# Neighbourhood attention in column order of the grid, inside a one-core backbone kernel

## The chip, the cores and the metric

The kernel runs on one core of a Trainium2 chip, as one program with one launch. The metric is device time in microseconds. Its profile comes from one more execution, recorded by the hardware's profiler.

The core's engines run side by side and meet at semaphores: TensorE (PE, with its weight loads listed as PEld), VectorE (DVE), ScalarE (ACT), GpSimd (POOL) and SyncE (SP), which issues most DMAs. A DMA can also be issued from ACT's queue. Each engine takes its instructions in the order in which they were written. TensorE writes its results to eight banks, each of 128 partitions by 512 fp32 values; the other engines read them from there.

## The reference, cut to what matters

A backbone of two layers works on 256 latent tokens (a grid of 4 rows by 64 columns), 256 context tokens and a width of 2048. Layer 0 has 16 attention heads of 128 and 32 state-space (SSD) heads side by side, then one output projection; layer 1 is a gated short convolution. The change is in the attention of layer 0. With 4 rows the row window of 8 holds all rows, so a query sees 16 of 64 columns, in each of the 4 rows, and all of the context:

```python
def neighbourhood_attention(q, k, v, k_ctx, v_ctx, rpb):
    ...
    kh = min(NA_KH, rows)
    col_start = jnp.clip(col - NA_KW // 2, 0, GRID_W - NA_KW)
    in_win = (col[None, :] >= col_start[:, None]) & (col[None, :] < col_start[:, None] + NA_KW)
    ...
    def row_block(r):
        ...
        s_lat = jnp.einsum('bqhd,bkhd->bhqk', qr, kb).astype(jnp.float32) * scale + bias.astype(jnp.float32)
        s_lat = jnp.where(mask, s_lat, -jnp.inf)
        s_ctx = jnp.einsum('bqhd,bkhd->bhqk', qr, k_ctx).astype(jnp.float32) * scale
        pr = jax.nn.softmax(jnp.concatenate([s_lat, s_ctx], axis=-1), axis=-1).astype(v.dtype)
        return (jnp.einsum('bhqk,bkhd->bqhd', pr[..., :kh * GRID_W], vb)
                + jnp.einsum('bhqk,bkhd->bqhd', pr[..., kh * GRID_W:], v_ctx))
```

The bias comes from a table `rpb` by row and column distance. Queries and keys are normalised per head first; the output is multiplied by a SiLU gate.

## The kernel before, in words

All products are made of three matmuls: each fp32 operand is split into a high part in the rounded format fp32r and a low part (the remainder), and high x high, high x low and low x high are added in a bank. Weights stream from memory through five buffers `raw` of 512 KB. ScalarE casts the high half (L420), VectorE subtracts the low half (L427), into one of three places `w`; later in the kernel further buffers serve as places too. A load is issued on SP (L381, L383) when a `raw` buffer comes free, in the order of the list of loads; between them go the loads of `adaT`, rows of the modulation matrix that VectorE multiplies (L823).

The order of the work is made by a planner in the kernel. The projections are written out as a fixed sequence of matmuls. Everything else is a generator that yields, before each step, the engine and the tiles that it needs; after each small group of matmuls `pump()` emits those steps whose inputs and engine are ready by the planner's own estimates. There are three queues: `urgent` (turning, gates, SSD inputs), `side` (heads and SSD groups, in the order in which they were put there) and `back` (the modulation). So a step that is moved shifts others.

Attention runs in four blocks of four heads (a = 0 to 3). `do_qk` projects queries (256 latent tokens, two tiles of 128) and keys (512 tokens: four tiles, two latent and two context). `kq_gen` normalises them and turns them with TensorE, tile by tile, four heads to a bank (L199); ScalarE copies the high part out of the bank (L994, L998), VectorE makes the low part (L996, L1000). Tokens keep their order, row by row. `v_gen` copies the projected values, tile by tile, to `Vt` (L1012).

`head_gen` is one head. It loads the bias from a table `rpbs` that was spread out in DRAM at the start, with four small DMAs (L1039), and adds the column mask (L1044). For each of two query tiles, `score` makes three matmuls of 512 columns (all 256 latent and 256 context keys; L195 is the line of every matmul). `top` adds bias and finds the maximum (L1057), ScalarE takes the exponential (L1062), `scale_` divides (L1067). TensorE turns the probabilities; their high and low parts go to `PH` and `PL` (L1099, L1101). The head's values are split into `VH` and `VL` (L1110, L1112), and twelve matmuls of 256 columns (four key tiles by three) give the output, which is multiplied by the gate (L1122). `put_mix` sends it to DRAM, or directly to the high and low buffers `mix` of the output projection (L944, L946) when that is near. `mix_gen` fetches those that went to DRAM back (L1561, L1562).

After block a come the SSD projections of two groups, `do_ssd(a)`; its group steps are `group_gen`. Block 3 differs: its gates and values are projected after `do_ssd(3)`, directly ahead of the output projection, whose first use of the last four heads' outputs (mix 12 to 15) is at the end of its first pass.

Of the kernel before, what the change touches and what calls it, by code (L numbers as in the profile page):

```python
# [31 lines left out]
for _name, _w in (("ident", 128), ("sel", 2), ("mhalf", 32), ("strip", 384), ("mask", 64)):  # L32
    _coff[_name] = (_n, _n + _w)
    _n += _w
# [107 lines left out]
def kernel(ctx: ExitStack, tc, x, cx, ada0, w0, adaT, w_in, w_out, sc_in, sc_out, rpb, small, const,  # L142
# [209 lines left out]
    ident, strip, mask, mhalf = C_("ident"), C_("strip"), C_("mask"), C_("mhalf")  # L352
# [200 lines left out]
    for a in range(1, 4):  # L553
        qk = [(w_in, CQ(a), 512), (w_in, CK(a), 512)]
        gv = [(w_in, CG(a), 512), (w_in, CV(a), 512)]
        for j_ in qk + gv + ssd_cols(a) if a < 3 else qk + ssd_cols(a) + gv:
            q_proj(*j_)
# [356 lines left out]
    got.add(("V", 0))  # L914
# [13 lines left out]
    rpbs = drt([16, 64, 320], "rpbs")  # L928
    E(DMA.dma_start(rpbs, bass.AP(tensor=rpb.tensor, offset=76, ap=[[465, 16], [0, 64], [1, 320]])))
    dcol = P_("dcol")  # L930
    for b_ in bias:
        E(G.memset(b_[:, 2, :], 0.0))
# [26 lines left out]

    def kq_gen(key, a, ps, nt, stat, dst, low, banked):  # L960
# [23 lines left out]
        for t in range(nt):  # L984
            yield W_("PE", kns[t], nb=1)
            pt = bank()
            for h in range(4):
                turn(pt[:, h * 128:(h + 1) * 128], kns[t][:, h * 128:(h + 1) * 128])

            o = slice(t * 128, (t + 1) * 128)  # L990
            yield W_("ACT", pt)
            if key == "K":
                give(free_t, kns[t])
                E(S.copy(dst[:, :, o], four(pt)))  # L994
                yield W_("DVE", dst[:, :, o])
                E(V.tensor_tensor(out=low[:, :, o], in0=four(pt), in1=dst[:, :, o].bitcast(F32), op=ALU.subtract))  # L996
            else:
                E(S.mul(dst[:, :, o], four(pt), gqk))  # L998
                yield W_("DVE", dst[:, :, o])
                E(V.scalar_tensor_tensor(out=low[:, :, o], in0=four(pt), scalar=gqk, in1=dst[:, :, o].bitcast(F32),  # L1000
                                         op0=ALU.mult, op1=ALU.subtract))
                give(free_t, kns[t])
            give(free_b, pt)
        got.add((key, a))

    def v_gen(a, ps):
        yield when(lambda: not (attn[0] < 8 * a))
        for t in range(4):

            on_dve = a == 3 and t % 2  # L1010
            yield W_("DVE" if on_dve else "ACT", ps[t])
            E(V.tensor_copy(Vt[:, t, :], ps[t]) if on_dve else S.copy(Vt[:, t, :], ps[t]))  # L1012
            give(free_b, ps[t])
        got.add(("V", a))
# [14 lines left out]
    b0 = rpbs[0, :, :]  # L1029
# [3 lines left out]
    def head_gen(a, h):  # L1033
# [4 lines left out]
        for r in range(4):  # L1038
            E(DMA.dma_start(bt[64 * (r % 2):64 * (r % 2) + 64, r // 2, :].rearrange("p (a b) -> p a b", a=4),  # L1039
                            bass.AP(tensor=b0.tensor, offset=b0.offset + hd * 64 * 320 + (7 - r) * 31 - 61,  # L1040
                                    ap=[[319, 64], [31, 4], [1, 64]])))
        yield W_("DVE", bt)
        bv = bt[:, 0:2, :].rearrange("p q (r c) -> p (q r) c", c=64)
        E(V.tensor_tensor(out=bv, in0=bv, in1=mask.unsqueeze(1).to_broadcast([128, 8, 64]), op=ALU.add))  # L1044
        sps = {}

        def score(qt):
# [3 lines left out]
            mm(ps, QT[:, h, o], KL[:, h, :], False, False)  # L1051
            mm(ps, QL[:, h, o], KT[:, h, :], False, True)
            return ps

        def top(qt, ps):
            sp = sps[qt] = tmp()
            E(V.tensor_tensor_reduce(out=two(sp), in0=two(ps), in1=bt[:, 1:3, :] if qt else bt[:, 0::2, :], scale=1.0,  # L1057
# [4 lines left out]
            E(S.activation(sp, sp, AF.Exp, bias=s4[:, 2 + qt:3 + qt], scale=1.0, accum_out=s4[:, 4 + qt:5 + qt]))  # L1062

        def scale_(qt):
            sp = sps[qt]
# [49 lines left out]
        for kt in range(4):  # L1115
            mm(po[:, :256], VH[:, kt], PH[:, kt, :], kt == 0, False)
            mm(po[:, :256], VH[:, kt], PL[:, kt, :], False, False)
            mm(po[:, :256], VL[:, kt], PH[:, kt, :], False, kt == 3)
# [3 lines left out]
        E(V.tensor_tensor(out=o, in0=po[:, :256], in1=gt[:, h, :], op=ALU.mult))  # L1122
# [358 lines left out]
    Btm[0] = st([128, 2, 4, 128], "Btm", name="Btmt")  # L1481
    spawn(urgent, kq_gen("K", 0, parK, 4, statk, KT, KL, False), 4)
    spawn(urgent, kq_gen("Q", 0, psQ, 2, statq, QT, QL, True), 2)

    def do_g(a, nxt):
        psG = banks(2)
        proj(512, 256, psG, nxt)
        spawn(urgent, silu2_gen("G", a, psG, gt, lambda: attn[0] >= 8 * a and (a or ("K", 0) in got)), 1)
# [34 lines left out]
    def do_qk(a, nxt):  # L1523
# [6 lines left out]
        for h in range(4):  # L1530
            spawn(side, head_gen(a, h))

    def do_gv(a, nxt):
        do_g(a, 4)
# [9 lines left out]
    do_ssd(3, 2)  # L1544


    def mix_gen(ip):
# [11 lines left out]
        for j, i in enumerate(pair):  # L1559
            hl = st([128, 2, 256], f"hH{i}" if i < 16 else f"hL{i - 16}", F32R, name=f"mix{i}")  # L1560
            E(S.copy(hl[:, 0], m3[:, j]))  # L1561
            E(V.tensor_tensor(out=hl[:, 1], in0=m3[:, j], in1=hl[:, 0].bitcast(F32), op=ALU.subtract))  # L1562
# [490 lines left out]
```

## Time and profile before

| | |
|---|---|
| median of 3 runs | 1765.8 us (1763.58 to 1766.23) |
| the profiled execution | 1760.31 us |
| its span, first to last instruction | 1758.5 us |
| PE busy | 1736.7 us, 99% |
| DVE busy | 1223.6 us, 70% |
| ACT busy | 773.4 us, 44% |
| mean granted TensorE clock | 0.999 |
| DMA | 377.66 MB, mean 215 GB/s |

Busy time is the time in which at least one instruction of an engine runs. A matmul's row gives its own length, into which the next one already runs, so the rows' lengths add up to more than the busy time. Idle time of an engine stands with what ended it. A wait in the list of waits is that idle time, by pairs of who waited and who released. Numbers at the end of a name (bank, tmp) are left out in the profile's rows.

### The profile page before, as it was taken

What the parts mean: (1) busy time and instruction counts of PE and PEld (TensorE: products, weight loads), DVE (VectorE), ACT (ScalarE), POOL (GpSimd) and SP (SyncE); (2) the same over time, 40 slices, a digit from 0 to 9 for tenths busy, and PEclk for the clock granted to TensorE, in tenths of its full rate; (3) what the DMA queues carried; (4) which work ended last, traced back from release to release, by engine and by line L of the source; (5) the groups of instructions that cost most, each with busy time, mean ns of one, the idle gap of its engine ahead of it and who ended that gap; (6) DMA issues with size and microseconds to landing.
All of it is one profiled execution on the core that took longest, in us unless ns stands there. A gap on an engine that the chain in (4) does not pass through costs nothing.

```text
span 1758.5 us, 25025 instructions
## 1 busy us (share of the span) xinstructions
PE 1736.7 (99%) x9451; PEld 1463.1 (83%) x9451; DVE 1223.6 (70%) x1978; ACT 773.4 (44%) x1330; POOL 31.6 (2%) x28
## 2 busy tenths in 40 slices
PE   6999999999999999999999999999999999999998
PEld 4777988889888889888888898888888888888887
DVE  5666887878685878686877787787668555555554
ACT  5333544445242436343435343564446444444442
POOL 0000100001000000000000000000000000000000
PEclk9999999999999999999999999999999999999999
DMA  9987644686756767656776557768767666666563
GB/s 362 342 307 258 209 143 138 183 246 191 234 165 195 219 205 227 210 175 210 220 213 193 166 185 255 246 221 284 274 222 228 195 188 192 192 191 188 190 208 121
DMA packets 202536, 377.66 MB, mean 215 GB/s; under 512 B 32384, under 2 KB 69040, under 8 KB 202416
## 3 DMA queue, kind: packets, MB, share of 16 engines
q1 hardware_dynamic: 195152, 369.49, 65.5%
q10 hardware_dynamic: 7264, 6.58, 1.1%
q8 instruction: 74, 1.21, 0.3%
q14 instruction: 46, 0.38, 0.1%
HBM read 370.62 MB, written 6.71 MB: 215 GB/s over the span
## 4 chain that ended last, share of the span: by engine, by line
PE 94%; DMA 2%; DVE 2%; issue 1%; ACT 0%; POOL 0%; SPq 0%; ACTq 0%; DVEq 0%; POOLq 0%
PE bank L195 91%; PE bank L199 3%; DMA tmp<-dram_csr 1%; DVE w L427 1%; DMA raw<-in_ada 0%; DMA tmp<-dram_exr 0%; DMA raw<-in_adaT 0%; DVE tmp L1235 0%; ACT w L420 0%; POOL statk L572 0%; DVE mix L1562 0%; SPq L583 0%; DVE raw L823 0%; DVE tmp L603 0%; DVE Vt L1012 0%
## 5 line engine op out<-in xcount | busy, mean ns | idle before, releaser
L420 ACT CAST w<-raw 128x1024 fp32r<-128x1024 f32 x343 | 359.5, 1049 | 530.4 <-PE bank L195 447.7
L427 DVE TENSOR_TENSOR w<-raw,w 128x1024 fp32r<-128x1024 f32 x343 | 416.6, 1217 | 231.4 <-ACT w L420 230.1
L195 PE MATMUL bank<-hH,w 128*128 128x256 f32 (+1 forms) x2064 | 488.0, 324 | 1.2 <-DVE w L427 1.1
L195 PE MATMUL bank<-w,hH 128*128 128x512 f32 x1280 | 407.4, 396 | 2.7 <-ACT hH L757 2.5
L195 PEld LDWEIGHTS bank<-hH,w 128*128 128x128 f32 x2064 | 344.7, 188 | 34.2 <-DVE w L427 2.1
L195 PE MATMUL bank<-hL,w 128*128 128x256 f32 (+1 forms) x1040 | 334.3, 321 | 0.0
L195 PEld LDWEIGHTS bank<-w,hH 128*128 128x128 f32 x1280 | 237.7, 189 | 54.4 <-issue 4.0
L195 PE MATMUL bank<-w,hL 128*128 128x512 f32 x640 | 249.9, 391 | 0.1
L195 PEld LDWEIGHTS bank<-hL,w 128*128 128x128 f32 x1040 | 196.3, 189 | 14.9
L195 PE MATMUL bank<-w,h 128*128 128x512 f32 x768 | 179.7, 390 | 0.0
L823 DVE CUSTOM_DVE_ANT_0 raw<-raw,csb 128x1024 f32<-128x1024 f32 x128 | 155.4, 1219 | 26.2 <-DMA raw<-in_adaT 24.0
L195 PEld LDWEIGHTS bank<-w,h 128*128 128x128 f32 x768 | 143.6, 188 | 29.6
L195 PEld LDWEIGHTS bank<-w,hL 128*128 128x128 f32 x640 | 120.5, 188 | 25.4 <-DVE hL L763 0.6
L195 PE MATMUL bank<-w,mix 128*128 128x512 f32 x588 | 138.3, 391 | 0.9 <-DVE w L427 0.9
L195 PEld LDWEIGHTS bank<-w,mix 128*128 128x128 f32 x588 | 109.5, 188 | 24.0 <-DVE w L427 1.3
L1235 DVE SCALAR_TENSOR_TENSOR tmp<-bank,cwh,tmp 128x508 f32<-128x508 f32 (+1 forms) x96 | 71.0, 744 | 1.8
L195 PE MATMUL bank<-KL,h 128*128 128x512 f32 x264 | 63.8, 389 | 0.0
L427 DVE TENSOR_TENSOR KL<-raw,KL 128x1024 fp32r<-128x1024 f32 x32 | 39.1, 1223 | 33.1 <-ACT KL L420 33.1
L427 DVE TENSOR_TENSOR wL<-raw,wH 128x1024 fp32r<-128x1024 f32 x31 | 37.9, 1224 | 33.5 <-ACT wH L420 33.4
L427 DVE TENSOR_TENSOR QL<-raw,QT 128x1024 fp32r<-128x1024 f32 x32 | 39.2, 1224 | 29.8 <-ACT QT L420 29.8
L195 PEld LDWEIGHTS bank<-KL,h 128*128 128x128 f32 x264 | 49.5, 188 | 10.2
L195 PE MATMUL bank<-QT,h 128*128 128x512 f32 x168 | 56.2, 391 | 0.0
(291 smaller groups left out, 1984.7 us busy)
## 6 DMA issues: line engine op xcount, KB each, us to landing
raw<-in_w_in SPq DMA_DIRECT2D x196, 512.0 KB, 3.9
raw<-in_adaT SPq DMA_DIRECT2D x128, 512.0 KB, 4.8
raw<-in_sc_in SPq DMA_DIRECT2D x128, 512.0 KB, 3.8
raw<-in_w_out SPq DMA_DIRECT2D x64, 512.0 KB, 5.0
raw<-in_ada SPq DMA_DIRECT2D x34, 512.0 KB, 6.9
raw<-in_sc_out SPq DMA_DIRECT2D x32, 512.0 KB, 4.1
PT<-in_ada SPq DMA_DIRECT2D x16, 512.0 KB, 6.9
raw<-in_w SPq DMA_DIRECT2D x16, 512.0 KB, 6.1
```

The costliest lines, as they stand in the source:

```text
L195: E(T.matmul(o, l, r, start=start, stop=stop, skip_group_check=True))
L199: E(T.transpose(o, i, ident if k == 128 else ident[:k, :k]))
L420: E(S.copy(H, v))
L427: E(V.tensor_tensor(out=Lo, in0=v, in1=H.bitcast(F32), op=ALU.subtract))
L823: E(V.tensor_tensor_reduce(out=raw, in0=raw, in1=csb, scale=1.0, scalar=0.0, op0=ALU.mult, op1=ALU.add, accum_out=gp[:, h, m:m + 1]))
L1235: E(V.scalar_tensor_tensor(out=do, in0=di, scalar=cwh[:, 32 * k + ch:32 * k + ch + 1], in1=do, op0=ALU.mult, op1=ALU.add))
```

## The change

Tokens are ordered column by column of the grid inside attention (token = 4 x column + row), so that a tile of 128 queries is 32 columns by 4 rows. The keys a tile can see then lie in 40 neighbouring columns, 160 tokens, and the key order becomes: latent columns 0 to 31, context, latent columns 32 to 63. Tile 0 needs keys 0 to 415 of 512, tile 1 needs 96 to 511.

- `kq_gen` turns the two latent tiles of two heads into one bank, and writes them in the new order: two runs of 64 elements with a step of four elements. Context tiles are turned as before.
- The values' latent tiles go to DRAM in two pieces each and come back in the new order (`turn_v`, `turned_v`), on SP; for block 0 this runs right after the first projections (`first_v`).
- Scores have 416 columns. The 96 others of the probabilities are set to zero by VectorE. In the value products two of four key tiles have 160 columns.
- The bias table is laid out by the host in the final order, one load of 128x672 per head; the mask is added in three pieces.
- The heads of block 3 are put into `side` after SSD groups 6 and 7, not before them.
- In `mix_gen` the low part is a step of its own.

How that shows in the engines' order. On TensorE, where the keys of block 0 are turned while the gates are projected (`hH` times `w`; `tmp` holds normalised keys, `const` the identity), before:

```order
L195 MATMUL bank_84<-hH_994,w_97 128x256
L199 MATMUL bank_88<-const,tmp_65 128x128 x4
L195 MATMUL bank_82<-hH_994,w_97 128x256
L195 MATMUL bank_82<-hL_999,w_97 128x256
L195 MATMUL bank_82<-hH_994,w_97 128x256 x2
L195 MATMUL bank_82<-hL_999,w_97 128x256
L195 MATMUL bank_82<-hH_994,w_97 128x256
L199 MATMUL bank_85<-const,tmp_73 128x128 x4
L195 MATMUL bank_84<-hH_1096,w_95 128x256
```

And now:

```order
L195 MATMUL bank_82<-hH_994,w_97 128x256
L199 MATMUL bank_88<-const,tmp_65 128x2x64
L199 MATMUL bank_88<-const,tmp_73 128x2x64
L199 MATMUL bank_88<-const,tmp_65 128x2x64
L199 MATMUL bank_88<-const,tmp_73 128x2x64
L199 MATMUL bank_85<-const,tmp_65 128x2x64
L199 MATMUL bank_85<-const,tmp_73 128x2x64
L195 MATMUL bank_84<-hH_1096,w_95 128x256
```

The two banks are filled behind one another once both tiles are normalised, four turns in each, instead of one bank per tile.

On TensorE in the output projection's first pass, at the last heads (`mix` is the projection's left side, KT and QT are scores, PH and VH value products), before:

```order
L195 MATMUL bank_83<-KL,QT 128x512
L195 MATMUL bank_83<-KT,QL 128x512
L195 MATMUL bank_88<-w_96,mix_8971 128x512 x3
L195 MATMUL bank_86<-w_97,mix_9045 128x512 x3
L195 MATMUL bank_89<-w_97,mix_9045 128x512 x3
L195 MATMUL bank_86<-w_97,mix_9048 128x512 x3
L195 MATMUL bank_89<-w_97,mix_9048 128x512 x3
L195 MATMUL bank_84<-w_95,mix_9045 128x512 x3
L195 MATMUL bank_87<-PH,VH 128x256
```

And now:

```order
L195 MATMUL bank_82<-PH,VL 128x256
L195 MATMUL bank_82<-PH,VH 128x160
L195 MATMUL bank_82<-PL,VH 128x160
L195 MATMUL bank_82<-PH,VL 128x160
L195 MATMUL bank_83<-w_95,mix_9227 128x512 x3
L195 MATMUL bank_87<-KT,QT 128x416
L195 MATMUL bank_87<-KL,QT 128x416
L195 MATMUL bank_87<-KT,QL 128x416
```

Scores and value products are narrower, and the last head's scores come later: 66 matmuls stand between the last value product and the first use of mix 12, where 174 stood.

On SP, at the values of block 3 in the same pass (`raw` are weight loads, `csr` rows of the SSD groups), before:

```order
L383 DMA raw_91<-in_w_out 128x2x512
L383 DMA raw_94<-in_w_out 128x2x512
L1039 DMA bias_159<-dram_rpbs 64x4x64 x4
L383 DMA raw_93<-in_w_out 128x2x512
L1039 DMA bias_160<-dram_rpbs 64x4x64 x4
L1391 DMA tmp_65<-dram_csr 128x2x256
```

And now:

```order
L383 DMA raw_94<-in_w_out 128x2x512
L960 DMA dram_vd<-Vt 64x512 x4
L383 DMA raw_92<-in_w_out 128x2x512
L1432 DMA tmp_72<-dram_csr 128x2x256
L1432 DMA tmp_71<-dram_csr 128x2x256
L383 DMA raw_91<-in_w_out 128x2x512
L383 DMA raw_93<-in_w_out 128x2x512
L965 DMA Vt<-dram_vd 128x2x512
```

The values' writes and their read now stand among the weight loads, and the bias loads of block 3 (one per head) stand elsewhere.

The diff, cut to its core:

```diff
+    vd = drt([256, 512], "vd")
...
+    def turn_v(t):
+        for r in range(2):
+            yield W_("SP", Vt[:, t, :])
+            E(DMA.dma_start(vd.rearrange("(c r) n -> c r n", r=4)[:, 2 * t + r, :], Vt[64 * r:64 * r + 64, t, :]))
+    def turned_v(a):
+        yield W_("SP", vd)
+        E(DMA.dma_start(Vt[:, 0:2, :], vd.rearrange("(t p) n -> p t n", p=128)))
+        got.add(("V", a))
...
     def kq_gen(key, a, ps, nt, stat, dst, low, banked):
...
-        for t in range(nt):
+        for hp in (0, 2):
+            yield W_("PE", kns[0], kns[1], nb=1)
+            pt = bank()
+            for k in range(2):
+                o = pt[:, k * 256:k * 256 + 256].rearrange("p (c r) -> p r c", r=4)
+                for t in range(2):
+                    turn(o[:, 2 * t:2 * t + 2, :], kns[t][:, (hp + k) * 128:(hp + k + 1) * 128])
...
+        for t in range(2, nt):
             yield W_("PE", kns[t], nb=1)
...
     def v_gen(a, ps):
...
+            if t == 1:
+                for k in range(2):
+                    yield from turn_v(k)
+        yield from turned_v(a)
...
+    BLOCKS = ((1, 2, slice(0, 256)), (2, 3, slice(0, 256)), (0, 0, slice(0, 160)), (3, 1, slice(96, 256)))
...
     def head_gen(a, h):
...
-        for r in range(4):
-            E(DMA.dma_start(bt[64 * (r % 2):64 * (r % 2) + 64, r // 2, :].rearrange("p (a b) -> p a b", a=4),
...
+        bf = bt.rearrange("p a b -> p (a b)")[:, :672]
+        E(DMA.dma_start(bf, rpb[hd]))
...
-            mm(ps, QT[:, h, o], KT[:, h, :], True, False)
+            mm(ps[:, :416], QT[:, h, o], KT[:, h, k_], True, False)
...
+            E(V.memset(sp[:, 0:96] if qt else sp[:, 416:512], 0.0))
...
-        for kt in range(4):
-            mm(po[:, :256], VH[:, kt], PH[:, kt, :], kt == 0, False)
+        for i, (kt, vt, q_) in enumerate(BLOCKS):
+            mm(po[:, q_], VH[:, vt], PH[:, kt, q_], i == 0, False)
...
     def do_qk(a, nxt):
...
-        for h in range(4):
+        for h in range(4 if a < 3 else 0):
             spawn(side, head_gen(a, h))
...
     do_ssd(3, 2)
+    for h in range(4):
+        spawn(side, head_gen(3, h))
...
     def mix_gen(ip):
...
             E(S.copy(hl[:, 0], m3[:, j]))
+            yield W_("DVE", hl[:, 0])
             E(V.tensor_tensor(out=hl[:, 1], in0=m3[:, j], in1=hl[:, 0].bitcast(F32), op=ALU.subtract))
```

More of the change, by code (lines that the diff above doesn't have):

```diff
@@ L31 @@
 _n = 0
-for _name, _w in (("ident", 128), ("sel", 2), ("mhalf", 32), ("strip", 384), ("mask", 64)):
+for _name, _w in (("ident", 128), ("sel", 2), ("mhalf", 16), ("mid", 16), ("strip", 384), ("mask", 64)):
     _coff[_name] = (_n, _n + _w)
@@ L988, in kq_gen @@
                 turn(pt[:, h * 128:(h + 1) * 128], kns[t][:, h * 128:(h + 1) * 128])
-            o = slice(t * 128, (t + 1) * 128)
+            o = slice(t * 128 - 128, t * 128)
             yield W_("ACT", pt)
[L992 to L1002, printed above, removed]
+            give(free_t, kns[t])
+            E(S.copy(dst[:, :, o], four(pt)))
+            yield W_("DVE", dst[:, :, o])
+            E(V.tensor_tensor(out=low[:, :, o], in0=four(pt), in1=dst[:, :, o].bitcast(F32), op=ALU.subtract))
             give(free_b, pt)
```

91 lines of the change are left out of this document (62 added, 29 removed).

## The prediction

> **What bounds the kernel now.** I read the page first (busy shares and chain), then the list of TensorE's own waits, then groups of instructions by shape, then narrow timelines.
>
> ```profile
> span 1758.5 us, 25025 instructions
> PE 1736.7 (99%) x9451; PEld 1463.1 (83%) x9451; DVE 1223.6 (70%) x1978; ACT 773.4 (44%) x1330; POOL 31.6 (2%) x28
> PE 94%; DMA 2%; DVE 2%; issue 1%; ACT 0%; POOL 0%; SPq 0%; ACTq 0%; DVEq 0%; POOLq 0%
> ```
>
> TensorE (PE) is busy 99% of the span and is 94% of the chain that ended last. What it waits for, in total and longest:
>
> ```profile
> PE bank L195 <- DMA raw<-in_ada: 10.8, 1, 10.8
> PE bank L195 <- ACT hH L757: 2.5, 2, 1.4
> PE bank L195 <- DVE w L427: 2.0, 3, 0.9
> PE bank L199 <- ACT half L724: 1.0, 2, 0.5
> PE bank L199 <- ACT x L613: 0.3, 1, 0.3
> PE bank L199 <- POOL r L1664: 0.3, 1, 0.3
> PE bank L195 <- DVE gt L789: 0.2, 1, 0.2
> ```
>
> The first two, the fourth and the fifth rows are the opening (first load, first norm). The change starts after it, with the first turning of keys near 208 us. So behind the opening at most about 2.5 us of named waiting is left to win (2.0 + 0.3 + 0.2), and the time follows the matmuls that PE must issue. What one costs is its distance to the next, not its length in a row (matmuls overlap). One long run of 512 columns, from the chain, and one of 256, from busy time by stretches:
>
> ```profile
> 1235.80 68.75 PE bank L195 x303
> 297.91:320.03 22.12, 21.93 (x193) 1.00 0.50 149
> ```
>
> 512 columns: 68.75/303 = 0.227 us. 256 columns: 22.12/193 = 0.115 us, at a granted clock of 1.00. The difference is 0.112 us per 256 columns, 0.44 ns per column.
>
> **The change part by part.** Scores. Each of 16 heads has two query tiles of three matmuls, 96 in all, and their moving side shrinks from 512 to 416 columns.
>
> ```profile
> L195 PE MATMUL bank<-KT,QT 128*128 128x512 f32 x32 | 13.1, 408 | 0.0
> L195 PE MATMUL bank<-KT,QL 128*128 128x512 f32 x32 | 12.5, 391 | 0.0
> L195 PE MATMUL bank<-KL,QT 128*128 128x512 f32 x32 | 12.5, 391 | 0.0
> ```
>
> 96 columns x 0.44 ns = 42 ns less each, x 96 = 4.0 us. All of it is on PE's path, and 416 columns (0.185 us) stay far above the 0.115 us that shorter matmuls reach anyway.
>
> Values. Each head has 12 matmuls of 256 columns; six become 160 wide, 96 in all.
>
> ```profile
> L195 PE MATMUL bank<-PL,VH 128*128 128x256 f32 x64 | 17.9, 280 | 0.0
> 402.18 0.53 PEld L195 LDWEIGHTS bank<-const,half 128*128 128x128 f32 x4
> 402.63 0.19 PEld L195 LDWEIGHTS bank<-hH,w 128*128 128x128 f32 x1
> ```
>
> By columns alone a 160-wide one would take 0.073 us: another 42 ns x 96 = 4.0 us. But each matmul also has its own weight load. The second and third rows show four loads for matmuls of one single column: they start 402.18 to 402.63, 0.45 us for four, 0.112 us apart, although almost nothing is streamed. If PV's loads are as slow, a 160-wide matmul cannot follow sooner than 0.112 us, and the gain is 96 x 3 ns = 0.3 us. Ends: 0.3 and 4.0 us. I take 0.3, since these loads are the nearest row (the same 128x128 of 4 bytes, at the same clock).
>
> [...]
>
> Turning. Keys and queries are turned by as many 128-column instructions as before (16 for keys, 8 for queries in each of 4 blocks). But 64 of them (32 for latent keys, 32 for queries) now write two runs of 64 elements with a step of four elements in the bank. No matmul of the old trace writes with a step, so the price is unknown.
>
> ```profile
> 1235.36 0.44 PE bank L199 x4
> L199 PE MATMUL bank<-const,tmp 128*128 128x128 f32 x356 | 50.5, 272 | 0.0
> ```
>
> A packed turn takes 0.44/4 = 0.11 us. Ends: 0 (same pace; a gain has no reason, as the elements stay 128), and 64 x 0.11 = 7.0 us if each takes twice as long. I take 0: a turn delivers 128 elements in 0.11 us, 1.2 per ns, half the 2.2 per ns of the 256-column stream above, so the bank is written with room to spare.
>
> VectorE and ScalarE. The score reduction (L1057, 32 times, 0.685 us at 512 elements) loses 96 elements, the scaling (0.487 us) and the exponential as well. Against it stand 32 zero fills of 96 elements and 32 more, smaller, additions of the mask.
>
> ```profile
> L1057 DVE CUSTOM_DVE_ANT_0 tmp<-bank,bias 128x512 f32<-128x512 f32 x16 | 11.0, 686 | 2.5 <-PE bank L195 2.5
> L1067 DVE TENSOR_SCALAR tmp<-tmp,s 128x512 f32<-128x512 f32 x32 | 15.6, 487 | 1.1
> L1044 DVE TENSOR_TENSOR bias<-bias,const 128x512 f32<-128x512 f32 x16 | 11.0, 685 | 0.5 <-DMA bias<-dram_rpbs 0.5
> L1122 DVE TENSOR_TENSOR half<-bank,gt x16: 408/423/425, 270.9 to 1170.2; 128x256 f32<-128x256 f32 x16
> L1060 DVE TENSOR_SCALAR s<-s x32: 153/154/156, 253.1 to 1155.1; 128x1 f32<-128x1 f32 x32
> ```
>
> From 0.685 at 512 and 0.423 at 256 an element costs 1.02 ns with a fixed 0.16. Reductions: 32 x 0.098 = -3.1 us. Scaling: (0.487-0.154)/511 x 96 x 32 = -2.0. Mask: per head 0.29+0.23+0.29 instead of 0.685, +2.0 in all. Fills: between 0.154 and 0.26 us each, +4.9 to +8.3. Net +2 to +5 us on an engine that is idle 535 us. I cost it at nothing: what hides it is the ready weights, below. The split of copy and subtraction in the mixing step (L1561, L1562) lets VectorE do other work where it waited for ScalarE:
>
> ```profile
> 1118.16 0.76 DVE L1562 TENSOR_TENSOR mix<-tmp,mix 128x256 fp32r<-128x256 f32 x2 [0.88 <-ACT mix L1561]
> 1122.46 1.89 PE L195 MATMUL bank<-w,mix 128*128 128x512 f32 x7 [0.91 <-DVE w L427]
> ```
>
> The second row is one of the three waits of PE for VectorE, just behind such a stall. It may vanish or move: 0 to -0.9 us, and I take 0, because the new order packs the same work (value copies, mixing, group 3's scores) into the same stretch.
>
> Queues. SyncE (SP) issues the weights in order. It loses 64 bias loads and one table copy, and gains 16 bias loads (336 KB each), 16 writes (128 KB) and 4 reads (512 KB) of the turned values: 29 fewer.
>
> ```profile
> L1039 SPq DMA_DIRECT2D bias<-dram_rpbs x64: 573/614/2243, 223.6 to 1139.2; - x64
> dram_mixd<-half ACTq DMA_DIRECT2D x24, 128.0 KB, 3.1
> raw<-in_w_in SPq DMA_DIRECT2D x196, 512.0 KB, 3.9
> L1012 ACT COPY Vt<-bank x10: 573/590/608, 477.9 to 1120.8; 128x512 f32<-128x512 f32 x10
> ACT w L420 <- PE bank L195: 458.1, 223, 5.8
> SPq L383 <- DVE w L427: 601.5, 237, 7.0
> ```
>
> At 0.614 us an issue that frees about 18 us of SP, which no one waits for. The new risk is a wait in that queue: the writes wait for the value copies, the read waits for the writes (3.1 us by the nearest row, the same 128 KB), and all weight loads stand behind. In the order of group 3, three weight loads stand between writes and read, each for 12 matmuls of 0.227 = 2.7 us of PE work, so the writes have landed by then. And PE is covered: ScalarE waited 458 us for PE to hand back places, so split weights lie ready, and SP waited 601 us for free buffers, so loads run ahead. Cost 0; if the cover is gone, the 3.1 us of a landing come out as a wait of PE for a weight's low half (L427 of before).
>
> Last heads. Their scores now come behind the SSD groups, and group 3's values are late by the round trip (3.1 + 3.9 us, the row of a load of the same 512 KB, and queueing). In the order, 66 matmuls stand between the last value product and the first use of head 12's output, where there were 174: 66 x 0.227 = 15.0 us against a tail (product with the gate 0.42, copy, subtraction) of about 2 us. Cost 0; SSD outputs, which are used before them, gain the room.
>
> **The sum.** -4.0 - 0.3 = -4.3 us of PE. The profiled execution took 1760.3 us (1758.5 plus 1.8 around it) and would take 1756.0. It lies 5.5 us under the median of the runs, 1765.8, and by that median the forecast is 1761.5.
>
> **The rivals.**
> (a) Narrow value products do gain by columns: -8.0, 1757.8. Against it speaks the 0.112 us between loads; for it, that these loads feed another number format.
> (b) Writing with a step slows the 64 turns. Twice as long: +7.0 - 4.3 = +2.7, 1768.5. This is the one that can end slower: it decides from 7.8/7.0, an extra 1.1 times a turn's 0.11 us; three times as long gives +9.7, 1775.5. No row speaks for it; the pace of a turn, half the stream's, speaks against. [...]
> (c) The round trip or the late heads open waits of PE. It costs nothing until the values of group 3 are 13 us later than the order has them (15.0 - 2). From there each us late is a us of wait: 4.3 us eat the gain (1765.8), past 7.8 us it is slower, and if each of the four groups made PE wait out the 3.1 us of a landing, 12.4 us, it would be 1773.9. For it: a slack of 15 us where there was 39. Against: the 29 fewer issues and the ready weights.
> (d) The change saves nothing because other work fills the freed slots: 1765.8. Against it: PE is the chain, and the removed columns are its own.
>
> **How the numbers follow.** A change under 0.2% (3.5 us) can hardly be told from none here; the three runs shown span 2.7 us. Chances: the sum as it stands 0.48 (0.40 of it past 3.5 us, 0.08 short of it), (a) in part or full 0.15, (b) about twice 0.10, (b) beyond that 0.07, (c) small 0.06, (c) large 0.11, (d) 0.03. Faster 0.55, same 0.27, slower 0.18. The range reaches from 1756.5 ((a), with the one wait of 0.9 gone) to 1768.5 ((b) at twice).
>
> **What would show it.** In the profile after: score matmuls 128x416, with lengths about 42 ns under 391 (that is 349); value products of 160 columns that start about 0.112 us apart (a if near 0.073); groups of four stepped turns at 0.44 us (b if 0.9); TensorE's waits behind the opening still near 2.5 us, none naming the values or a weight load late behind L965 (c otherwise). The forecast is wrong if PE's busy time falls by 4 us and the span doesn't, or if the busy time itself doesn't fall.

## The result, and the profile after

The changed kernel takes 1759.7 us (median of 22 runs, 1756.5 to 1764.5), the kernel before on the same chip 1763.2 us (22 runs, 1760.1 to 1768.6). The ratio is 0.9976, 95% interval 0.9968 to 0.9984: 4.2 us less, a gain of 0.24% (by the interval 2.8 to 5.6 us; the two medians alone lie 3.5 us apart). The sum of the forecast was -4.3 us.

The profiled execution of the changed kernel says something else at first sight. Its page, with the span, the busy shares and the chain that ended last:

```profile
span 1759.6 us, 25036 instructions
PE 1733.2 (99%) x9451; PEld 1462.6 (83%) x9451; DVE 1218.6 (69%) x2042; ACT 768.1 (44%) x1330; POOL 31.4 (2%) x26
PE 94%; DMA 2%; DVE 2%; ACT 1%; issue 0%; SPq 0%; POOL 0%; DVEq 0%; ACTq 0%
```

The span is 1.1 us longer than that of the profile before (1758.5), while TensorE's busy time fell by 3.5 us (1736.7 to 1733.2). So in this pair of executions TensorE worked less and waited more. Its waits in the trace after (total us, times, longest us):

```profile
PE bank L195 <- DVE ssq L603: 10.8, 1, 10.8
PE bank L195 <- DVE w L427: 6.2, 5, 3.0
PE bank L195 <- ACT hH L757: 2.5, 2, 1.4
...
```

Row by row, with those left out (1.0 us and less), this is the list of before (the 10.8 us of the first load stand under another releaser), but for one: the waits for VectorE's low half of the weights (L427) went from 2.0 to 6.2 us. The longest, 3.0 us, lies at 679 us. The chain of work there (start, length, what):

```profile
672.92 6.64 DMA raw<-in_adaT
...
680.91 1.14 DVE w L427
...
682.09 3.03 PE bank L195 x18
```

and VectorE's step on the adaT tile, with its own idle time in brackets:

```profile
679.59 1.23 DVE L823 CUSTOM_DVE_ANT_0 raw<-raw,csb 128x1024 f32<-128x1024 f32 x1 [2.09 <-DMA raw<-in_adaT]
```

VectorE had reached the next step of the matrix-vector product (L823), whose adaT tile was 6.6 us in transfer, and stood there for 2.1 us; the weight half that TensorE needed (L427) is the next long step in its order. And the wait costs more than its 3.0 us. Busy time by stretches of the same trace (stretch, its length, busy us of TensorE with the number of matmuls, weight loads, VectorE, ScalarE, GpSimd, then the granted clock):

```profile
678.00:682.00 4.00, 1.14 (x10) 0.93 (x8) 2.41 (x5) 2.25 (x5) 1.01 (x1) 1.00 0.33 120
682.00:683.30 1.30, 1.21 (x10) 1.21 (x11) 1.30 (x3) 0.00 (x0) 1.30 (x1) 1.00 0.86 244
683.30:686.70 3.40, 3.40 (x19) 3.40 (x19) 2.90 (x5) 0.90 (x1) 1.49 (x1) 0.53 0.94 316
686.70:690.00 3.30, 3.30 (x30) 3.30 (x30) 2.78 (x5) 1.71 (x4) 0.00 (x0) 0.97 0.74 235
```

About 1.3 us after TensorE resumed, its clock was granted at 0.53 for 3.4 us: 19 matmuls where the next 3.3 us hold 30. That is another 1.3 us or so (3.40 - 19/30 x 3.30).

The steps of the forecast, in the same trace, by shape and by start:

```profile
L195 PE MATMUL bank<-KT,QT 128*128 128x416 f32 x32 | 11.8, 370 | 0.0
L195 PE MATMUL bank<-KL,QT 128*128 128x416 f32 x32 | 11.3, 352 | 0.0
L195 PE MATMUL bank<-KT,QL 128*128 128x416 f32 x32 | 11.2, 349 | 0.0
...
271.03 0.24 PE L195 MATMUL bank<-PH,VH 128*128 128x160 f32 x1
271.10 0.28 PE L195 MATMUL bank<-PL,VH 128*128 128x160 f32 x1
271.22 0.27 PE L195 MATMUL bank<-PH,VL 128*128 128x160 f32 x1
271.33 0.28 PE L195 MATMUL bank<-PH,VH 128*128 128x160 f32 x1
...
271.66 0.61 PE L199 MATMUL bank<-const,tmp 128*128 128x128 f32 x4
...
207.97 1.04 PE L199 MATMUL bank<-const,tmp 128*128 128x128 f32 x8
```

The score matmuls are 38 to 42 ns shorter than before. The second of the six narrow value products of a head starts 0.07 us after the first, the others 0.11 us apart; all six take 271.66 - 271.03 = 0.63 us. The eight turns that write with a step (the last row) take 1.04 us as a group, of which the last takes 0.27 by its own length, so they start 0.11 us apart, like packed ones.

So two questions went to the chip: whether the 4.2 us are the columns of the scores, and whose the waits are.

### The profile page after: what moved, and what is told of

Its sections match the earlier page's. It is cut to its first block, busy times and chain, and to the rows that moved or that the text cites. A ratio compares the mean times of both kernels' runs of the same rounds, so it can differ in the third digit from the quotient of the medians.

```text
span 1759.6 us, 25036 instructions
## 1 busy us (share of the span) xinstructions
PE 1733.2 (99%) x9451; PEld 1462.6 (83%) x9451; DVE 1218.6 (69%) x2042; ACT 768.1 (44%) x1330; POOL 31.4 (2%) x26
## 4 chain that ended last, share of the span: by engine, by line
PE 94%; DMA 2%; DVE 2%; ACT 1%; issue 0%; SPq 0%; POOL 0%; DVEq 0%; ACTq 0%
PE bank L195 90%; PE bank L199 3%; DMA tmp<-dram_csr 1%; DVE w L427 1%; DMA raw<-in_adaT 1%; DMA raw<-in_ada 0%; DVE raw L823 0%; DMA bias<-in_rpb 0%; ACT w L420 0%; DVE tmp L1456 0%; ACT tmp L1441 0%; DVE tmp L1445 0%; SPq L583 0%; ACT tmp L1451 0%; DVE tmp L759 0%
## 5 line engine op out<-in xcount | busy, mean ns | idle before, releaser
L420 ACT CAST w<-raw 128x1024 fp32r<-128x1024 f32 x343 | 359.1, 1049 | 519.9 <-PE bank L195 443.6
L427 DVE TENSOR_TENSOR w<-raw,w 128x1024 fp32r<-128x1024 f32 x343 | 416.5, 1218 | 232.9 <-ACT w L420 223.6
L195 PE MATMUL bank<-w,hH 128*128 128x512 f32 x1280 | 406.3, 395 | 2.7 <-ACT hH L757 2.5
L823 DVE CUSTOM_DVE_ANT_0 raw<-raw,csb 128x1024 f32<-128x1024 f32 x128 | 155.6, 1220 | 28.7 <-DMA raw<-in_adaT 23.0
L427 DVE TENSOR_TENSOR KL<-raw,KL 128x1024 fp32r<-128x1024 f32 x32 | 39.2, 1224 | 32.4 <-ACT KL L420 32.4
L427 DVE TENSOR_TENSOR QL<-raw,QT 128x1024 fp32r<-128x1024 f32 x32 | 39.2, 1224 | 29.4 <-ACT QT L420 29.3
L427 DVE TENSOR_TENSOR wL<-raw,wH 128x1024 fp32r<-128x1024 f32 x31 | 37.9, 1224 | 30.4 <-ACT wH L420 30.4
```

The lines of the kernel that those rows point to most:

```text
L195: E(T.matmul(o, l, r, start=start, stop=stop, skip_group_check=True))
L420: E(S.copy(H, v))
L427: E(V.tensor_tensor(out=Lo, in0=v, in1=H.bitcast(F32), op=ALU.subtract))
L823: E(V.tensor_tensor_reduce(out=raw, in0=raw, in1=csb, scale=1.0, scalar=0.0, op0=ALU.mult, op1=ALU.add, accum_out=gp[:, h, m:m + 1]))
```

## The experiments: what the parts are worth

All ratios are to the kernel before, on the same chip. In pv256, s512, pv32 and no_rt the planner was shown the operands and transfers of the changed kernel, so that every engine's remaining instructions stand in exactly its order; in packed they do so anyway, and before_s416 stands in the order of the kernel before. The argument by which a matmul shows the planner the old operands is left out of the diffs.

**s512: the scores wide again.**

```diff
-            mm(ps[:, :416], QT[:, h, o], KT[:, h, k_], True, False)
-            mm(ps[:, :416], QT[:, h, o], KL[:, h, k_], False, False)
-            mm(ps[:, :416], QL[:, h, o], KT[:, h, k_], False, True)
+            mm(ps, QT[:, h, o], KT[:, h, :], True, False)
+            mm(ps, QT[:, h, o], KL[:, h, :], False, False)
+            mm(ps, QL[:, h, o], KT[:, h, :], False, True)
...
-            E(V.tensor_tensor_reduce(out=two(sc), in0=two(ps[:, :416]), in1=b_, scale=1.0,
+            E(V.tensor_tensor_reduce(out=two(sc), in0=two(ps[:, span(qt)]), in1=b_, scale=1.0,
```

> The changed kernel with all 96 score products 512 columns wide again, of which the same 416 are read; every engine's instructions in the same order. If the gain is the 96 columns that each score product lost (96 x 96 x 0.44 ns), it is gone: +4.0 us, 1.000 of the kernel before (0.9990 to 1.0008). If the gain came from elsewhere (fewer waits, less VectorE work, less traffic), the time stays at 0.9976.

Measured: 0.9995 (0.9984 to 1.0005), 1762.5 us. The gain is gone. Its trace has the old lengths again (the line is one further down):

```profile
L196 PE MATMUL bank<-KT,QT 128*128 128x512 f32 x32 | 13.1, 411 | 0.0
L196 PE MATMUL bank<-KT,QL 128*128 128x512 f32 x32 | 12.5, 390 | 0.0
L196 PE MATMUL bank<-KL,QT 128*128 128x512 f32 x32 | 12.5, 390 | 0.0
```

Between 0.9976 and this lie 0.0019, 3.4 us; the forecast's 4.0 us would make 0.9999, inside the interval. The starts of matmuls say the same without the noise of whole runs: from the first score product of a query tile to the matmul behind the third, the 32 tiles take 22.5 us in the trace of before, 18.8 in that of the changed kernel and 22.5 in this one.

**before_s416: the scores narrow, alone.**

```diff
-            mm(ps, QT[:, h, o], KT[:, h, :], True, False)
-            mm(ps, QT[:, h, o], KL[:, h, :], False, False)
-            mm(ps, QL[:, h, o], KT[:, h, :], False, True)
+            mm(ps[:, :416], QT[:, h, o], KT[:, h, :416], True, False)
+            mm(ps[:, :416], QT[:, h, o], KL[:, h, :416], False, False)
+            mm(ps[:, :416], QL[:, h, o], KT[:, h, :416], False, True)
```

> The kernel before, with its 96 score products cut from 512 to 416 columns and nothing else (the last 96 keys are left out of the products; the softmax reads what stood in the bank); every engine's instructions stand in the order of the kernel before. If the columns are the gain, this alone gives it: 96 x 96 x 0.44 ns = 4.0 us, 0.9977 of the kernel before (0.9969 to 0.9986). If the gain needs the rest of the change, 1.000.

Measured: 0.9974 (0.9959 to 0.9989), 1758.4 us. The narrow scores alone, without turning, round trip, new biases or moved heads, give as much as the whole change. Taken back from the changed kernel they take the gain with them; given to the kernel before they bring it (18.5 us from start to start in its trace). That settles where the gain is, within the 2 to 3 us of each interval.

**pv256: the value products wide again.**

```diff
-            mm(po[:, q_], VH[:, vt], PH[:, kt, q_], i == 0, False)
-            mm(po[:, q_], VH[:, vt], PL[:, kt, q_], False, False)
-            mm(po[:, q_], VL[:, vt], PH[:, kt, q_], False, i == 3)
+            mm(po[:, :256], VH[:, vt], PH[:, kt, :], i == 0, False)
+            mm(po[:, :256], VH[:, vt], PL[:, kt, :], False, False)
+            mm(po[:, :256], VL[:, vt], PH[:, kt, :], False, i == 3)
```

> The changed kernel, with all twelve value products of a head 256 columns wide again (the weights are zero in the columns added, so nothing else changes); every engine's instructions stand in the same order as in the changed kernel. If a narrow value product is held up by its weight load (the forecast's term of -0.3 us; the changed kernel's trace, where the 96 products of 160 columns start 0.09 to 0.11 us apart, says up to -1.0), this gives back 0.3 to 1.0 us: 0.9978 to 0.9982 of the kernel before. If it is paid by columns (96 x 96 columns x 0.44 ns), it gives back 4.0 us: 0.9999.

Measured: 0.9977 (0.9966 to 0.9988), 1760.3 us. By the middles of the two ratios the narrow value products are worth 0.2 us, nothing that can be told from none; the 4.0 us of rival (a), which would make 0.9999, lie outside. The starts are finer: the six products of a head that are wide again take 0.69 to 0.72 us in this trace, where the narrow ones take 0.63 to 0.64, in all 16 heads. That is 0.065 us x 16, about 1.0 us.

**pv32: the narrow value products narrower still.**

```diff
+            a_ = slice(q_.start, q_.start + (256 if i < 2 else 32))
-            mm(po[:, q_], VH[:, vt], PH[:, kt, q_], i == 0, False)
+            mm(po[:, a_], VH[:, vt], PH[:, kt, a_], i == 0, False)
...
```

> The changed kernel with its 96 value products of 160 columns cut to 32 columns (this leaves out most of those products); every engine's instructions stand in the same order. If a narrow product takes as long as its weight load (0.11 us, whatever its width), the time stays within 1 us: 0.9970 to 0.9982 of the kernel before. If it is paid by columns (96 x 128 x 0.44 ns), 5.4 us go: 0.9945.

Measured: 0.9973 (0.9957 to 0.9988), 1758.6 us; 0.9945 is outside. The reason can be read in its trace, in the starts of the products of 32 columns:

```profile
271.92 0.18 PE L196 MATMUL bank<-PH,VH 128*128 128x32 f32 x1
271.94 0.26 PE L196 MATMUL bank<-PL,VH 128*128 128x32 f32 x1
272.06 0.26 PE L196 MATMUL bank<-PH,VL 128*128 128x32 f32 x1
272.17 0.26 PE L196 MATMUL bank<-PH,VH 128*128 128x32 f32 x1
...
272.50 0.65 PE L200 MATMUL bank<-const,tmp 128*128 128x128 f32 x4
```

The second comes 0.02 us after the first (0.07 at 160 columns). From there on they start 0.11 us apart, as the 160-wide ones do: each has its own weight load, and behind the second none follows sooner than 0.11 us, at 32 columns as at 160. A head's six take 0.58 us here, 0.05 less than at 160 columns, or 0.8 us in all.

**packed: the latent turns without the step.**

```diff
-                o = pt[:, k * 256:k * 256 + 256].rearrange("p (c r) -> p r c", r=4)
+                o = pt[:, k * 256:k * 256 + 256].rearrange("p (r c) -> p r c", r=4)
```

> The changed kernel with the 64 turns of the latent keys and queries written to 128 words in a row instead of to every fourth word (this leaves out their reordering into grid order; the work is otherwise the same, in the same order on every engine). If the step costs nothing, the time stays at 0.9976 of the kernel before (within 0.0008). If a stepped write makes a turn twice as long (64 x 0.109 us), this kernel is 7.0 us faster than the changed one: 0.9936; a cost of half that shows as 0.9956.

Measured: 0.9973 (0.9961 to 0.9985), 1758.9 us. The step costs nothing that can be told from none; a doubled turn (0.9936) is outside. Its first group of turns is as long as the stepped one shown above:

```profile
208.50 1.04 PE L199 MATMUL bank<-const,tmp 128*128 128x128 f32 x8
```

**no_rt: no round trip of the values.**

```diff
-            E(DMA.dma_start(vd.rearrange("(c r) n -> c r n", r=4)[:, 2 * t + r, :], Vt[64 * r:64 * r + 64, t, :]))
...
-        E(DMA.dma_start(Vt[:, 0:2, :], vd.rearrange("(t p) n -> p t n", p=128)))
```

> The changed kernel without the round trip of the latent values through DRAM (it leaves out their reordering: 16 stores and 4 loads on SP's queue); the order of all other instructions is that of the changed kernel. If the round trip is hidden, the time stays at 0.9976 of the kernel before, within 0.0008. If its stores and loads hold up the weight streams or the value products, and so feed the waits of PE behind VectorE that the changed kernel's trace shows (4.2 us more than before the change), this kernel is 2 to 4 us faster: 0.9953 to 0.9965.

Measured: 0.9987 (0.9975 to 1.0000), 1761.0 us. Nothing is gained without the 20 transfers; the middle is even above that of the changed kernel, with intervals that overlap. Its trace has 5.4 us of waits for VectorE's weight halves, so those waits are not the round trip's.

**heads_before: the last heads where they were.**

```diff
-        for h in range(4 if a < 3 else 0):
+        for h in range(4):
             spawn(side, head_gen(a, h))
...
-    for h in range(4):
-        spawn(side, head_gen(3, h))
```

> The changed kernel with the heads of the last block started ahead of the SSD groups, where the kernel before starts them. The forecast costed their move at nothing: 0.9976 of the kernel before, within 0.0008, up to the waits that a new order shifts (the changed kernel's trace has 9 us of short PE waits on VectorE behind late transfers, which may come or go with any new order: 2 us either way). If late heads cost by waits at the end, this is 2 us or more faster: below 0.9965. If their move is where the gain came from, it is slower: 0.9990 or more.

Measured: 0.9980 (0.9968 to 0.9992), 1759.8 us: no difference from the changed kernel. (The 9 us of the expectation are not in the list of waits of the changed kernel's trace: that has 6.2 for L427, this run's has 5.2.)

## The experiments: whose the waits are

**after_again and before_again: both kernels a second time, unedited, for a second trace of each.**

> The changed kernel itself, beside the two variants of this set, and to see how far its waits differ between two executions of one program. Every theory: 0.9976 of the kernel before, within 0.0010. If the 3.1 us wait at 679 us belongs to one execution (the variants with the same order showed 0.9 to 2.5 us there), this profile shows another length there; if it belongs to the order, 3 us again.

> The kernel before itself, for a second trace of it. Its first profiled execution (1760.3 us) lay 3 us under its median and showed 2.0 us of PE waits behind VectorE's weight splits, where eight executions of the changed order showed 2.0 to 6.2. If those waits are a cost of the changed order, this execution shows about 2 us again, whatever its time. If they vary from one execution to the next in the kernel before as well, this one, nearer the median, shows 4 us or more. Against itself: 1.000, within 0.001.

Measured: 0.9979 (0.9970 to 0.9988) for the changed kernel; 0.9998 (0.9987 to 1.0008) for the kernel before against itself. The waits for L427, first in the second trace of the changed kernel, with the same two steps near 679 us:

```profile
PE bank L195 <- DVE w L427: 4.0, 4, 1.7
...
678.66 1.23 DVE L823 CUSTOM_DVE_ANT_0 raw<-raw,csb 128x1024 f32<-128x1024 f32 x1 [2.00 <-DMA raw<-in_adaT]
...
681.16 0.50 PE L195 MATMUL bank<-hH,w 128*128 128x256 f32 x2 [1.00 <-DVE w L427]
```

then in the second trace of the kernel before (span 1767.6 us), with two stretches around its longest waits by busy time and clock (columns as above):

```profile
PE bank L195 <- DVE w L427: 4.0, 4, 1.5
PE bank L195 <- ACT w L420: 2.5, 2, 1.8
...
670.00:674.00 4.00, 1.86 (x13) 1.45 (x12) 3.76 (x8) 4.00 (x10) 0.00 (x0) 0.98 0.55 174
674.00:677.00 3.00, 3.00 (x22) 2.44 (x21) 2.97 (x6) 3.00 (x19) 0.00 (x0) 0.50 0.84 276
...
1126.00:1129.00 3.00, 0.57 (x2) 0.26 (x2) 3.00 (x6) 3.00 (x6) 0.00 (x0) 0.81 0.42 130
1129.00:1132.00 3.00, 3.00 (x7) 2.41 (x8) 3.00 (x7) 2.41 (x7) 0.00 (x0) 0.50 0.90 312
```

One program, two executions: the 3.0 us wait is one of 1.0 us the second time, and the clock stays at 1.00 (680 to 690 us). VectorE stood for the adaT tile both times, 2.1 and 2.0 us; but the second time it started on the tile 0.9 us earlier (678.66 against 679.59), and TensorE ran out of weights 1.0 us later (681.16 - 1.00 against 682.09 - 2.96). The kernel before, which showed 2.0 us of waits for weights in its first trace, shows 6.5 in its second, and twice a stretch at half clock (0.50) with them. So how long such a wait is belongs to the execution, and one pair of traces can't be read for it.

The place of a wait belongs to the order. The eight traces in the changed kernel's order up to there (after, after_again, no_rt, heads_before, packed, pv256, pv32, s512) all have VectorE standing 1.9 to 2.3 us for an adaT tile near 679 us (packed at 675) and TensorE waiting behind it, 0.7 to 3.0 us; all have VectorE waiting 0.8 to 1.8 us for a bias table near 408 us, with 0.5 to 2.3 us of TensorE waits behind it; and all have a TensorE wait of 0.7 to 0.8 us near 1150 us. The three traces in the order of before have one of 0.9 near 412 us, and others at places of their own: 0.9 us near 1122 in the first, 2.1 near 672 and 3.3 near 1127 in the second, none in before_s416. All waits for weights together come to 2.0 to 6.2 us in the eight, 4.5 in the mean, and to 2.0, 6.5 and 0.9 in the three, 3.1 in the mean. So the new order may cost a microsecond or so of waits; three traces don't show it, and the medians don't resolve it.

**late3, late_mix, late_all: VectorE's steps behind transfers emitted later.** If the waits come from VectorE standing behind late transfers, they must go when the planner, which writes every engine's order, expects those transfers later. (A variant with such a rule has another order on every engine, so it is no test of one wait alone.) late3 does so for the adaT tiles and the bias tables:

```diff
-            rdy += 4000 if eng == "PE" else 0
+            rdy += 4000 if eng == "PE" else 3000 if eng == "DVE" else 0
...
         E(DMA.dma_start(bf, rpb[hd]))
+        for k_ in plan.keys(bf):
+            plan.w[k_] += 3000.0
```

late_mix has this too and also

```diff
         E(DMA2.dma_start(m3[:, :n], mixd[i0:i0 + n].rearrange("b p c -> p b c")))
+        for k_ in plan.keys(m3[:, :n]):
+            plan.w[k_] += 4000.0
```

and late_all changes instead the planner's model of every transfer:

```diff
-                done = free = self.dma + 1000
+                done = free = self.dma + 3000
...
-                done = free = max(self.dma, s + 1000) + n / self.RATE + 2500
+                done = free = max(self.dma, s + 1000) + n / self.RATE + 5000
```

> The changed kernel with one more rule in the planner: VectorE's steps on the adaT tiles and on the bias tables are emitted only where the planner holds the transfer for 3 us longer done than it does now. Nothing else is edited, but every engine's order shifts with it. If the waits of PE behind VectorE (6.2 us in the changed kernel's trace, 2.0 to 5.2 us in those of its variants) come from VectorE standing in order behind late transfers, most of them go: 2 to 4 us less than the changed kernel, 0.9953 to 0.9965 of the kernel before. If they come from VectorE's load as such, the time stays at 0.9976 or rises.

> The variant late3 with the planner also holding the loads of the finished heads from DRAM on ScalarE's queue for 4 us longer. In late3's trace the waits near 410 and 679 us had shrunk to 0.7 us, but one of 2.4 us had come at 1113 us, behind an 8.6 us load of that kind. If each wait can be removed at its place, this one is 2 us less than late3: 0.996. If a shifted order brings another wait as often as it removes one, it stays at 0.9972, or rises.

> The changed kernel with the planner taking every transfer to land later than it does now (2 us on SP's queue, 2.5 us on ScalarE's), and nothing else edited. If the waits behind late transfers are the only thing left to gain beside the columns, 2 to 4 us less than the changed kernel: 0.9953 to 0.9965. If later emission leaves the weight splits less slack, new waits cost more than the old: above 0.998.

Measured: late3 0.9972 (0.9963 to 0.9982), 1759.0 us; late_mix 0.9954 (0.9940 to 0.9967, median of five), 1755.4 us; late_all 1.0168 (1.0153 to 1.0184), 1794.1 us.

late3 missed its range and can't be told from the changed kernel: the waits at 410 and 679 us went, but one of 2.2 us by the list of waits came at 1113 us, behind a load of finished heads. late_mix leaves 0.9 us at that place, and beats both kernels: 0.9954 against the 0.9979 of after_again in the same set, 4.4 us by the two ratios (3.3 by the medians), with intervals that don't overlap. The waits for weights that after_again lists and late_mix does not are 4.0 us. What VectorE waits for transfers of adaT, and TensorE's longest waits, first in after_again, then in late_mix (where no row of TensorE names L427 any more):

```profile
DVE raw L823 <- DMA raw<-in_adaT: 24.9, 25, 2.7
```

```profile
DVE raw L823 <- DMA raw<-in_adaT: 5.7, 9, 1.2
...
PE bank L195 <- DMA raw<-in_ada: 10.9, 1, 10.9
PE bank L195 <- ACT hH L757: 2.5, 2, 1.4
```

late_all shows the other side. With every transfer taken as later, everything behind a transfer is emitted later, the weight splits of the whole kernel with it. In its trace TensorE waits longer for VectorE, in more places, and the clock falls to 0.50 behind several of these waits (waits, then stretches):

```profile
PE bank L195 <- DVE w L427: 10.1, 5, 3.0
PE bank L195 <- DVE tmp L989: 4.7, 1, 4.7
PE bank L195 <- DVE VL L1151: 2.2, 1, 2.2
...
704.00:708.00 4.00, 0.26 (x1) 0.26 (x2) 2.37 (x4) 1.19 (x4) 2.96 (x1) 0.50 0.97 328
1230.00:1234.00 4.00, 1.23 (x5) 0.74 (x5) 2.06 (x6) 0.20 (x1) 1.62 (x1) 0.50 0.99 371
1234.00:1238.00 4.00, 3.74 (x9) 2.98 (x10) 0.98 (x3) 0.60 (x2) 0.00 (x0) 0.50 0.42 164
```

It is 35 us slower than the changed kernel beside it (1794.1 against 1758.8). That the late splits are the whole of it is argued from these rows, not shown, and no variant tried a smaller margin on all transfers.

## Why the prediction was right, and where it was not

**The sum.** -4.3 us forecast, -4.2 measured (0.9976; the interval is -2.8 to -5.6 us). That the two agree to 0.1 us is luck: one term was sized too small (the value products) and one put at nothing that may not be (the waits of the new order), in opposite directions. The forecast time, 1761.5, is 1.8 us above the measured median: the base moved by 2.6 (the three runs it stood on had a median of 1765.8, the 22 runs beside the changed kernel 1763.2), and the medians differ by 3.5 instead of 4.3. The lower end of the range, 1756.5, is 0.4 below what its own terms give (1757.8 - 0.9 = 1756.9).

**Scores, -4.0.** Right, and shown from both sides: s512 loses 3.4 us, before_s416 alone gains 4.6 (0.9974 of 1764.5). From start to start the traces give 3.8 (22.5 to 18.8 us), and 4.0 for before_s416. The spacing of long runs (0.44 ns per column) was the right price, and the lengths of 349 to 370 ns are where the forecast put them.

**Value products, -0.3 out of 0.3 to 4.0.** The floor was there, the size of the term too small: the starts give -1.0 us, which pv256's 0.2 (a difference of two ratios, each known to about 2 us) does not contradict. pv32 shows the floor: with a fifth of the columns a head's six products take 0.58 us instead of 0.63. The forecast took 0.112 us from the starts of the four loads for one-column matmuls; the four matmuls themselves, in the same window of the same trace, take 0.37 us from the first start to the next matmul (402.29 to 402.66), 0.093 each. Six narrow products in 0.63 us are 0.105 each. Their own loads, of rounded weights, start 0.11 us apart in the changed kernel's trace (271.03 to 271.48 us for five), like those for the one-column matmuls, so the other number format of rival (a) shows no gain there. That it is the load that holds the next product up stays the author's reading: no run changed the loads. Rival (a) falls: about a quarter of its 4.0 us is there.

**Turns with a step, 0 out of 0 to +7.0.** Right: packed and stepped groups have the same 1.04 us, and packed gains nothing that can be told. Rival (b) falls as it was put; a cost of a microsecond or two in all 64 turns the ratios could not show, but the two groups of 1.04 us show none.

**VectorE, +2 to +5 us, costed at 0.** The size was off; no run shows an effect on the time. The groups of the trace after:

```profile
L1096 DVE CUSTOM_DVE_ANT_1 tmp<-bank,bias 128x416 f32<-128x416 f32 x32 | 17.2, 538 | 2.9 <-PE bank L195 2.7
L1106 DVE TENSOR_SCALAR tmp<-tmp,s 128x416 f32<-128x416 f32 x32 | 14.0, 437 | 1.1
L1078 DVE TENSOR_TENSOR bias<-bias,const 128x128 f32<-128x128 f32 x32 | 9.1, 286 | 3.1 <-DMA bias<-in_rpb 3.1
L1093 DVE MEMSET tmp<- 128x96 f32 x32 | 4.4, 138 | 0.0
L1078 DVE TENSOR_TENSOR bias<-bias,const 128x64 f32<-128x64 f32 x16 | 3.5, 219 | 0.0
```

A reduction of 416 takes 538 ns, 147 less than the 685 of before (forecast 98 less): -4.7 us in all instead of -3.1. A fill takes 138 ns, under the lower end of 154: +4.4. With the scaling at -1.6 and the mask at +1.7 the net is about -0.2. The page's busy time, which counts overlaps once, fell by 5.0; part of that is the mask, whose three pieces per head overlap (0.63 us together, 0.79 by their own lengths), and the rest was not traced. What the forecast did not have is VectorE's wait for the new bias loads: 3.1 us (first row of L1078), where it waited 0.5 us for those of before.

**Queues and round trip, 0; last heads, 0; mixing, 0.** no_rt and heads_before are no faster than the changed kernel, so rival (c) falls as it was put: neither the round trip nor the late heads make TensorE wait. The forecast's argument was that split weights lie ready ahead of TensorE; near 408 and 679 us they don't, and there the new order has VectorE waiting for a bias load of 336 KB and for an adaT tile. No run took the new bias loads out, so their share stays open. The split in the mixing step was not tried by itself either; in the second trace of before VectorE waits for ScalarE twice by 0.88 us in that step (L1562), shortly ahead of TensorE's two waits of 3.3 us, and in the changed kernel's trace it does so once, by 2.2 us, with no wait of TensorE near it.

**The test the forecast set itself** failed: it called itself wrong if TensorE's busy time fell and the span did not, and in the pair of profiles that is about what happened (-3.5 and +1.1). The step behind it, that behind the opening at most about 2.5 us of waiting is left to win, took one execution for the kernel. Its profile lay 5.5 us under the median of the runs shown, and that was the sign; the second trace of the kernel before has 6.5 us of waits for weights alone and two stretches at half clock, and late_mix won 4.4 us from the changed kernel by an order in which VectorE stands much less behind late transfers (5.7 us for adaT instead of 24.9). A table by span shows what one pair is worth:

| execution | span, us | TensorE waits for weights (L420, L427), us | stretches at half clock behind the opening |
|---|---|---|---|
| before, first | 1758.5 | 2.0 | none |
| before, second | 1767.6 | 6.5 | two |
| after, first | 1759.6 | 6.2 | one |
| after, second | 1757.0 | 4.0 | none (170 to 1050 us) |
| late_mix | 1753.7 | none | none (170 to 1050 us) |

## What to carry to other kernels

Where TensorE is the chain, price a narrower matmul by the spacing of a long run, down to the spacing of matmuls with next to no columns (0.09 to 0.11 us here), and expect next to nothing below it (six products went from 0.63 us at 160 columns to 0.58 at 32); read that spacing from a whole group and the matmul behind it. Before reading a fraction of a per cent from two profiles, take a second one of each kernel: short waits behind late transfers changed their length here from one execution to the next (3.0 us, then 1.0), even where the order fixed their place, and behind some of them the clock fell (0.50 to 0.53). Where an engine works in an order written ahead, a step on a tile that may land late should not stand ahead of the step that the bottleneck waits for; but give the margin to that step alone: the one variant with a margin on all transfers was 35 us slower.

## What the runs showed of the hardware

A short wait of TensorE had an aftermath in some executions. After the single wait of 3.0 us in the first trace of the changed kernel the clock was granted at 0.53 for 3.4 us; in the second trace of the kernel before two waits close together (within 670 to 674 us TensorE was busy for 1.86 of 4.00 us) were followed by 0.50 as well. Behind waits of 2.2 to 2.4 us in late3, heads_before and no_rt the granted clock stayed at 1.00. So a single wait of 3.0 us was followed by a lower clock, and so was a stretch that was only about half idle.

The length of the wait alone did not decide it. In the opening all traces but late_all's have the same two waits for ScalarE's `hH`, 2.5 us together, the longer 1.4 and so the shorter 1.1. The shorter one ends at 23.35 us in the first trace of before and at 23.36 in that of after, and the first traces of the two kernels are alike up to there: TensorE is busy for 1.39 of the 3.00 us from 21 to 24 in both. Behind it the clock fell in one and not in the other (the rows of before, then of after):

```profile
24.00:28.00 4.00, 4.00 (x12) 2.93 (x11) 3.90 (x7) 3.58 (x8) 0.00 (x0) 0.58 1.01 402
24.00:28.00 4.00, 4.00 (x17) 2.69 (x17) 3.90 (x6) 3.65 (x8) 0.00 (x0) 1.00 1.02 404
```

It cost the kernel before 1.2 us (its next wait ends at 35.13 us, that of the changed kernel at 33.89). The matmuls of `w` and `hH` on 512 columns, which start there, are busy for 407.4 us in all in the first trace of before and for 406.3 in that of after. Of the other executions after_again, heads_before, pv256 and pv32 have 406.9 to 407.5, the second trace of before, before_s416, no_rt, packed, s512, late3 and late_mix 405.9 to 406.5; that the four had the low clock there too is an estimate from these sums. And heads_before, with TensorE busy for only 0.77 of the 3.00 us from 679 to 682, kept its clock (1.00 to 688 us). What else decides the runs do not show.
